# A planner's clock with other constants, and another order of the first loads, in an fp32 encoder kernel

## The chip, the cores and the metric

The kernel runs on one core of a Trainium2 chip. The metric is the device time of one execution in microseconds (us). The core has five engines that run side by side, each strictly in the order of its own program: TensorE (PE) multiplies matrices, with PEld for the loading of its stationary operand; VectorE (DVE) and ScalarE (ACT) do elementwise work; GpSimd (POOL) computes here only powers for norms; SyncE (SP) issues almost all DMAs. An engine waits for another by semaphores.

## What is computed

Two layers of an encoder, 256 tokens wide 1024, everything in fp32:

```python
def hybrid_layer(x, mem, ...):
    h = rms_norm(x, norm_mix_g)
    rq, rk, rv, rg, pv, nq, nk, nv, mq = jnp.split(h @ w_in, 9, axis=-1)
    ret = merge_heads(rms_norm(bidirectional_retention(rotary(rq), rotary(rk), rv), ret_norm_g)) * silu(rg)
    pool = multiscale_pool(pv, pool_w, pool_scale)
    na = neighbourhood_attention(rms_norm(nq), rms_norm(nk), nv, na_rpb)
    mk, mv = jnp.split(rms_norm(mem, norm_mem_g) @ w_mem_kv, 2, axis=-1)
    mo = memory_attention(rms_norm(mq), rms_norm(mk), mv)
    up = jnp.einsum('bsnc,ncd->bsnd', jnp.stack([ret, pool, na, mo], axis=2), w_branch)
    gates = sigmoid(h @ w_gate).reshape(b, s, N_BRANCH, dm)
    x = x + jnp.einsum('bsnd,bsnd->bsd', gates, up) @ w_out
    a, g = jnp.split(rms_norm(x, norm_ffn_g) @ w_ffn_in, 2, axis=-1)
    return x + (silu(a) * g) @ w_ffn_out
```

Each branch has 4 heads (or groups) of 64. The memory has 256 tokens.

## The kernel before

**Tiles.** The tokens are two tiles of 128 (t = 0, 1). Activations are turned (transposed on PE against an identity) so that they can be the stationary operand, and split in a high part, rounded by a cast to `fp32r`, and the low rest: `hhi`/`hlo` for normalized x, `bhi`/`blo` for branches, memory and the FFN's hidden block. Weights come as 272 slots of 512 KB (128 x 1024 fp32) and are split in the same way: ACT casts `raw` to `whi` (called a cast or a split below), DVE subtracts to get `wlo`. A product of two such pairs is three matmuls of 128x512, hi·hi, hi·lo and lo·hi, called three products below. A slot makes six products for each tile, in PSUM banks `A` (four) and `B` (two); `C` (two) is for turns. There are 4 `raw` buffers and 10 of each split. A slot's DMA is issued, on SP, right behind the subtraction that frees its `raw` buffer.

**Work beside the products.** The attention, retention, pooling, norm and FFN chains are Python generators. A chain issues a few instructions on ACT, DVE, POOL and PE (turns, scores, value products), then yields until its results are there. Among their steps: `to_heads` (about line 549) turns the heads of two sources into `C` and makes `ls`, `rs`, `rl` of them; `attention` makes scores in `B`, takes exponentials on ACT into `sc`, scales and turns them back (copies to `pt` for the first two heads, to `sc` for the second two), and multiplies with the values; `gate_chain` is a sigmoid on ACT; `hid_chain` (line 860) is a sigmoid on ACT and two DVE products, and `hid_T` turns the hidden block.

**What sets the order.** Nothing is ordered at run time. While the program is built, a model clock (class `Clock`, line 66) walks along: every instruction that is issued through the wrapper `Engine` gets a modelled start (after its operands, from a table of last reads and writes) and a modelled duration (`cost`, line 84). The main loop (line 1088) asks this clock which tile's next slot is `ready`; `background` resumes the chains whose time has come; `pump` (line 301) issues a slot's split when its weights have landed by the clock and when ACT or DVE is no more than a few microseconds behind PE by the clock. So the clock's constants decide in which place each cast, copy, sigmoid and turn stands in the order of its engine, and the chip then runs these orders as they are.

Before, the clock counts a product of 512 columns at 0.4167 ns a column and 13.5 ns, a transfer at 390 bytes per ns with 1.2 us ahead and 1.0 behind, 1.28 us for each change between exponential and sigmoid on ACT, and 0.2 us for each change of PE between its narrow fp32 products and others.

**The start** (`begin`, line 1007, and the lines from 1071) is written by hand. SP loads half of tile 0's x, slot 0 in two halves, slot 1, and so on; ACT's queue loads the identity and the first half of tile 1's x. PE runs some products on zeros, turns four blocks of tile 0, does the six products of slot 0 for tile 0, turns four blocks of tile 1, and does the six of slot 0 for tile 1.

Of the kernel before, what the change touches and what calls it, by code (L numbers as in the profile page):

```python
# [9 lines left out]
F32 = mybir.dt.float32  # L10
F32R = mybir.dt.float32r
AF = mybir.ActivationFunctionType
# [11 lines left out]
HD = 64  # L24
# [9 lines left out]
LEAD = 7  # L34
MAX_LAG = 8
WARM = 6.6
TABLE_LOAD = 1.28
WINDOW = (6, 4, 1.5, 0.4)
VERBOSE = False
BRANCHES = (2, 3, 0, 1)  # L40
# [3 lines left out]
class Engine:  # L44


    def __init__(self, real, clock, name):
        self.real, self.clock, self.name = real, clock, name

    def __getattr__(self, op):  # L50
        f = getattr(self.real, op)

        def call(*args, **kw):
            outs = [kw[k] for k in ("out", "accum_out") if kw.get(k) is not None]
            ins = [v for k, v in kw.items() if k not in ("out", "accum_out")]
            rest = list(args)
            if "out" not in kw:
                outs.append(rest.pop(0))
            func = next((v for v in rest if isinstance(v, AF)), None)
            self.clock.enter(self.name, op, outs, [v for v in ins + rest if isinstance(v, bass.AP)], kw, func)  # L60
            return f(*args, **kw)  # L61

        return call


class Clock:
# [5 lines left out]
    def __init__(self):  # L72
        self.at = dict.fromkeys(("PE", "ACT", "DVE", "POOL", "SP", "DMA"), 0.6)
        self.reads, self.writes = {}, {}
        self.mark = 0.0
        self.column = None
        self.narrow = False
        self.table = None

    @property  # L80
    def now(self):
# [2 lines left out]
    def cost(self, eng, op, outs, ins, kw):  # L84
        n = max([x.free_size() for x in outs[-1:] + ins[:1]])
        if eng == "PE":
            o = outs[0]
            n = o.free_size() * (2 if self.now < WARM else 1)
            narrow = op == "matmul" and ins[0].dtype == F32 and o.partition_size() == HD
            change = 0.2 * (narrow != self.narrow)  # L90
            self.narrow = narrow
            if op == "transpose":
                return n * 0.845e-3 + change
            if ins[0].dtype == F32R:
                return n * 0.4167e-3 + 0.0135 + change
            half = o.partition_size() == HD and o.base_partition()
            if o.partition_size() == HD:
                pair, self.column = self.column, None if half else n
                if half and pair == n:
                    return 0.02  # L100
            return max(n, 128) * 1.67e-3 + change
        if eng == "ACT":
            return 0.1 + n * 0.83e-3 + 0.1 * (kw.get("accum_out") is not None) + 0.04 * isinstance(kw.get("scale"), bass.AP)
        if eng == "POOL":
            if op == "memset":
                return 0.1 + n * 1e-3
            return 0.3 + 0.17 * n
        if op in ("tensor_copy", "tensor_scalar", "tensor_scalar_mul", "tensor_scalar_add", "memset"):
            return 0.085 + n * 0.6e-3
        return 0.08 + n * 1.045e-3 + 0.05 * (op == "scalar_tensor_tensor")  # L110

    def span(self, x):
        (stride, parts), *free = x.ap
# [12 lines left out]
        old = [r for r in table.get(key, ()) if r[4] > end - 60 and not (p0 <= r[0] and r[1] <= p1 and lo <= r[2] and r[3] <= hi)]  # L126
        table[key] = old + [(p0, p1, lo, hi, end, eng)]

    def enter(self, eng, op, outs, ins, kw, func=None):
        ins = [x for x in ins if x.space != bass.MemoryType.DRAM]  # L130
        outs = [x for x in outs if x.space != bass.MemoryType.DRAM]
        skip = "PE" if eng == "PE" else None
        t = max([self.last(self.writes, x) + self.LATENCY for x in ins]
                + [self.last(self.reads, x, eng) + self.LATENCY for x in ins if x.space == bass.MemoryType.PSUM]
                + [max(self.last(self.writes, x, skip), self.last(self.reads, x, skip)) + self.LATENCY for x in outs] + [self.at[eng]])
        if func in (AF.Exp, AF.Sigmoid) and func != self.table:
            self.table = func
            self.at["ACT"] += TABLE_LOAD
            t = max(t, self.at["ACT"])
        if op == "dma_start":  # L140
            self.at[eng] = t + 0.45
            t = max(self.at["DMA"], t + 1.2) + (outs + ins)[0].nbytes() / 390e3
            self.at["DMA"] = t
            end = t + 1.0
        else:
            end = self.at[eng] = t + self.cost(eng, op, outs, ins, kw)
        for x in ins:
            self.note(self.reads, x, end, eng)
        for x in outs:
            self.note(self.writes, x, end, eng)  # L150
        self.mark = max(self.mark, end)
# [9 lines left out]
def tile_encoder(ctx: ExitStack, tc: tile.TileContext, a: dict, out: bass.AP):  # L161
    clock = Clock()
    nc = Timed(tc.nc, clock)
# [184 lines left out]
    def start(gen, *reads):  # L348

        hold(*reads)  # L350
        chains.append([clock.now, gen])
# [655 lines left out]
    def begin():  # L1007

        parts = {(0, 0): (C[0], (0, 1)), (0, 1): (B[1], (2, 3)), (1, 0): (C[1], (0, 1)), (1, 1): (A[3], (2, 3)),
                 (0, 2): (C[0], (4, 5, 6, 7)), (1, 2): (C[1], (4, 5, 6, 7))}  # L1010

        def turn(t, *which):
            for c in which:
                bank, ks = parts[t, c]
                for i, k in enumerate(ks):
                    nc.tensor.transpose(bank[:, i * P:(i + 1) * P], X[t][:, k * P:(k + 1) * P], ident)

        def split(t, c):
            bank, ks = parts[t, c]
            ks = [(bank[:, i * P:(i + 1) * P], GAIN[0][0][:, k:k + 1], *act_h(t, k)) for i, k in enumerate(ks)]  # L1020
            for ps, g, hi, lo in ks:
                nc.scalar.activation(hi, ps, AF.Copy, scale=g)
            for ps, g, hi, lo in ks:
                nc.vector.scalar_tensor_tensor(out=lo, in0=ps, scalar=g, in1=hi.bitcast(F32), op0=ALU.mult, op1=ALU.subtract)
            if c:
                raise_flag(f"h{t}@0c{c - 1}")

        def weights():
            split_hi()
            split_lo()  # L1030

        state["by_hand"] = True
        warm(6)
        turn(0, 0, 1)
        warm(2)
        split(0, 0)
        weights()
        emit(0)
        turn(1, 0, 1)
        split(0, 1)  # L1040
        split(1, 0)
        emit(1)
        weights()
        split(1, 1)
        turn(0, 2)
        emit(0)
        turn(1, 2)
        split(0, 2)
        weights()
        emit(1)  # L1050
        split(1, 2)
        weights()
        emit(0)
        emit(1)
        state["by_hand"] = False
# [6 lines left out]
    with tc.manual_schedule():  # L1062
# [4 lines left out]
        def load_x(queue, t, c):  # L1067
            queue.dma_start(out=X[t][:, HALVES[c]], in_=a["x"][0, t * P:(t + 1) * P, HALVES[c]])
# [3 lines left out]
        load_x(nc.sync, 0, 0)  # L1072
        nc.scalar.activation(small[0], mhalf, AF.Square)
        clock.at["ACT"] += 1.2
        load_x(nc.scalar, 1, 0)
        issue_dmas(2)
        load_x(nc.sync, 0, 1)
        issue_dmas(3)
# [103 lines left out]
```

## Time and profile before

| | |
|---|---|
| three runs | 843.17 us median, 842.88 to 847.2 |
| profiled execution | 841.89 us, span 840.0 us |
| bytes moved | 152.86 MB, mean 182 GB/s |
| DVE, subtractions of weights | 275, 330.2 us busy |
| ACT, casts of weights | 273, 284.1 us busy |
| granted TensorE clock | 1.0 of full in the whole span |

The profile names operands by the program's names without buffer numbers; all compute stands under line 61, the wrapper's call. In the timeline a row has start, duration, engine, operation, output<-inputs, and in brackets the idle time of that engine just before, with what ended it. A row of PE longer than the distance to the next one is pipelining: the start of the next matmul, not the end of this one, shows the pace. An arrow in the view of waits reads "who waited <- for whom". A time against a name is when PE or an engine could not go on; idle time of ACT or DVE alone costs nothing.

### The profile page before, as it was taken

Reading aid. Unit: us, or ns where it says so; the run is one execution under the profiler, and the core shown is the slowest. Engines: PE = TensorE matmul, PEld = TensorE weight load, DVE = VectorE, ACT = ScalarE, POOL = GpSimd, SP = SyncE. Lnnn points to the kernel's source line nnn. Section 1 sums busy time; section 2 is a strip of 40 time slices with the busy share of each in tenths; the row PEclk is TensorE's granted clock in tenths of the full one; section 3 lists DMA queues with packets and bytes.
Section 4 is the critical chain, followed back from the end, with each engine's and each line's share of the span. In section 5 each row is a group of like instructions: output and inputs, shape, how many; then the busy total and the mean of one; then the engine's idle time right before and its main releaser. Section 6 shows DMA issues by size and latency. Waiting matters only on the chain.

```text
span 840.0 us, 10795 instructions
## 1 busy us (share of the span) xinstructions
PE 820.8 (98%) x3928; PEld 672.4 (80%) x3928; DVE 552.2 (66%) x802; ACT 470.1 (56%) x726; POOL 30.5 (4%) x32
## 2 busy tenths in 40 slices
PE   8999999999999999999999998999999999999998
PEld 6788778778887888888888877887888878888886
DVE  5898786865677556555568868584775765655541
ACT  6858887445465444444469677754444654444430
POOL 0400100000000000000011001000000000000000
PEclk9999999999999999999999999999999999999999
DMA  8946765546568656566374477446544676666611
GB/s 257 323 140 203 240 199 166 166 147 197 176 180 255 191 180 197 176 198 185 95 220 137 156 246 219 147 126 226 178 157 120 200 228 198 187 187 186 189 52 51
DMA packets 103765, 152.86 MB, mean 182 GB/s; under 512 B 6432, under 2 KB 55328, under 8 KB 103712
## 3 DMA queue, kind: packets, MB, share of 16 engines
q1 hardware_dynamic: 102848, 151.30, 57.1%
q10 hardware_dynamic: 864, 0.88, 0.3%
q8 instruction: 31, 0.51, 0.2%
q14 instruction: 22, 0.18, 0.1%
HBM read 151.10 MB, written 1.05 MB: 181 GB/s over the span
## 4 chain that ended last, share of the span: by engine, by line
PE 78%; ACT 7%; DMA 7%; DVE 6%; issue 2%; POOL 0%; SPq 0%; DVEq 0%; ACTq 0%; POOLq 0%
PE A L61 49%; PE B L61 25%; PE C L61 4%; DVE wlo L61 3%; ACT whi L61 2%; DMA raw<-in_w_in 2%; DMA mem<-in_pool_a 2%; DMA raw<-in_w_ffn_out 1%; DMA raw<-in_w_gate 1%; DVE w L61 1%; ACT rs L61 1%; ACT sc L61 1%; DMA raw<-in_w_mem_kv 1%; ACT qk L61 1%; ACT bhi L61 1%
## 5 line engine op out<-in xcount | busy, mean ns | idle before, releaser
L61 DVE TENSOR_TENSOR wlo<-raw,whi 128x1024 fp32r<-128x1024 f32 (+1 forms) x275 | 330.2, 1212 | 190.9 <-ACT whi L61 190.3
L61 ACT CAST whi<-raw 128x1024 fp32r<-128x1024 f32 (+1 forms) x273 | 284.1, 1050 | 214.0 <-PE A L61 83.0
L61 PE MATMUL A<-whi,hhi 128*128 128x512 f32 (+1 forms) x544 | 213.9, 393 | 1.6 <-ACT whi L61 0.7
L61 PE MATMUL A<-wlo,hhi 128*128 128x512 f32 (+1 forms) x544 | 208.9, 384 | 1.0 <-DVE wlo L61 1.0
L61 PE MATMUL A<-whi,hlo 128*128 128x512 f32 (+1 forms) x544 | 209.1, 384 | 0.0
L61 PEld LDWEIGHTS A<-whi,hhi 128*128 128x128 f32 x544 | 102.3, 188 | 23.2 <-issue 2.6
L61 PEld LDWEIGHTS A<-whi,hlo 128*128 128x128 f32 x544 | 102.2, 188 | 21.2 <-DVE hlo L61 0.8
L61 PEld LDWEIGHTS A<-wlo,hhi 128*128 128x128 f32 x544 | 102.5, 188 | 20.1 <-DVE wlo L61 2.0
L61 PE MATMUL B<-whi,hlo 128*128 128x512 f32 x288 | 112.5, 391 | 0.1
L61 PE MATMUL B<-whi,hhi 128*128 128x512 f32 x288 | 112.3, 390 | 0.0
L61 PE MATMUL B<-wlo,hhi 128*128 128x512 f32 x288 | 112.1, 389 | 0.0
L61 PE MATMUL A<-whi,bhi 128*128 128x512 f32 x272 | 108.3, 398 | 0.0
L61 PE MATMUL A<-whi,blo 128*128 128x512 f32 x272 | 106.2, 390 | 0.0
L61 PE MATMUL A<-wlo,bhi 128*128 128x512 f32 x272 | 106.1, 390 | 0.0
L61 PEld LDWEIGHTS B<-whi,hlo 128*128 128x128 f32 x288 | 54.0, 188 | 12.9 <-DVE hlo L61 1.8
L61 PEld LDWEIGHTS B<-wlo,hhi 128*128 128x128 f32 x288 | 54.1, 188 | 11.3
L61 PEld LDWEIGHTS B<-whi,hhi 128*128 128x128 f32 x288 | 54.1, 188 | 11.0
L61 PEld LDWEIGHTS A<-whi,blo 128*128 128x128 f32 x272 | 51.1, 188 | 11.0
L61 PEld LDWEIGHTS A<-whi,bhi 128*128 128x128 f32 x272 | 51.1, 188 | 10.4 <-issue 0.8
L61 PEld LDWEIGHTS A<-wlo,bhi 128*128 128x128 f32 x272 | 51.2, 188 | 9.7
L61 DVE SCALAR_TENSOR_TENSOR w<-B,rms,w 128x256 f32<-128x256 f32 x72 | 34.7, 482 | 3.9 <-ACT w L61 2.6
L61 ACT CAST bhi<-C 128x512 fp32r<-128x512 f32 x28 | 16.4, 586 | 34.4 <-PE C L61 34.3
(115 smaller groups left out, 605.5 us busy)
## 6 DMA issues: line engine op xcount, KB each, us to landing
raw<-in_w_ffn_in SPq DMA_DIRECT2D x176, 256.0 KB, 3.2
raw<-in_w_gate SPq DMA_DIRECT2D x64, 512.0 KB, 4.4
raw<-in_w_ffn_out SPq DMA_DIRECT2D x44, 512.0 KB, 3.9
raw<-in_w_in SPq DMA_DIRECT2D x35, 512.0 KB, 4.3
raw<-in_w_branch SPq DMA_DIRECT2D x16, 512.0 KB, 4.5
raw<-in_w_out SPq DMA_DIRECT2D x16, 512.0 KB, 4.2
raw<-in_w_mem_kv SPq DMA_DIRECT2D x8, 512.0 KB, 4.3
xn<-in_bias SPq DMA_DIRECT2D x4, 512.0 KB, 5.4
```

The source lines that it names most:

```text
L61: return f(*args, **kw)
```

## The change

The clock loses its two change costs (the function tables of ACT, narrow products of PE), counts a 512-column product at 0.416 ns a column and 3 ns, a transfer at 280 bytes per ns with 1.1 us ahead and 0.9 behind, 0.48 us instead of 0.45 for a DMA's issue, and DVE's fixed parts at 70 ns instead of 80 or 85. At the start, the first half of tile 1's x goes to SP's queue, behind both halves of slot 0, and its four turns stand between the third and the fourth product of tile 0.

```diff
@@ Clock.cost
-            narrow = op == "matmul" and ins[0].dtype == F32 and o.partition_size() == HD
-            change = 0.2 * (narrow != self.narrow)
-            self.narrow = narrow
             if op == "transpose":
-                return n * 0.845e-3 + change
+                return n * 0.84e-3
             if ins[0].dtype == F32R:
-                return n * 0.4167e-3 + 0.0135 + change
+                return n * 0.416e-3 + 0.003
...
-            return max(n, 128) * 1.67e-3 + change
+            return max(n, 128) * 1.67e-3
...
-            return 0.085 + n * 0.6e-3
-        return 0.08 + n * 1.045e-3 + 0.05 * (op == "scalar_tensor_tensor")
+            return 0.07 + n * 0.55e-3
+        return 0.07 + n * 1.05e-3 + 0.05 * (op == "scalar_tensor_tensor")
@@ Clock.enter
-        if func in (AF.Exp, AF.Sigmoid) and func != self.table:
-            self.table = func
-            self.at["ACT"] += TABLE_LOAD
-            t = max(t, self.at["ACT"])
         if op == "dma_start":
-            self.at[eng] = t + 0.45
-            t = max(self.at["DMA"], t + 1.2) + (outs + ins)[0].nbytes() / 390e3
+            self.at[eng] = t + 0.48
+            t = max(self.at["DMA"], t + 1.1) + (outs + ins)[0].nbytes() / 280e3
             self.at["DMA"] = t
-            end = t + 1.0
+            end = t + 0.9
@@ begin
         weights()
+        def between():
+            turn(1, 0, 1)
+            return
+            yield
+        start(between())
         emit(0)
-        turn(1, 0, 1)
         split(0, 1)
@@ first loads
-        load_x(nc.scalar, 1, 0)
-        issue_dmas(2)
+        issue_dmas(1)
+        load_x(nc.sync, 1, 0)
+        issue_dmas(2)
```

`emit` runs the chains after the first of its two groups of three products, and so `between` puts the turns there.

What this does to the orders is shown at three places. The first is PE's start, before: `x_105` and `x_106` are tiles 0 and 1 of x, `A_61` and `A_63` their banks, `whi_73`/`wlo_83` slot 0.

```order
L61 MATMUL B_65<-w_125 128x128 x2
L61 MATMUL A_61<-whi_73,hhi_93 128x512
L61 MATMUL A_61<-wlo_83,hhi_93 128x512
L61 MATMUL A_61<-whi_73,hlo_95 128x512
L61 MATMUL A_61<-whi_73,hhi_93 128x512
L61 MATMUL A_61<-wlo_83,hhi_93 128x512
L61 MATMUL A_61<-whi_73,hlo_95 128x512
L61 MATMUL C_68<-ident_gain,x_106 128x128 x2
L61 MATMUL A_64<-ident_gain,x_106 128x128 x2
L61 MATMUL A_63<-whi_73,hhi_94 128x512
```

And with the change:

```order
L59 MATMUL B_65<-w_125 128x128 x2
L59 MATMUL A_61<-whi_73,hhi_93 128x512
L59 MATMUL A_61<-wlo_83,hhi_93 128x512
L59 MATMUL A_61<-whi_73,hlo_95 128x512
L59 MATMUL C_68<-ident_gain,x_106 128x128 x2
L59 MATMUL A_64<-ident_gain,x_106 128x128 x2
L59 MATMUL A_61<-whi_73,hhi_93 128x512
L59 MATMUL A_61<-wlo_83,hhi_93 128x512
L59 MATMUL A_61<-whi_73,hlo_95 128x512
L59 MATMUL A_63<-whi_73,hhi_94 128x512
```

The four turns of tile 1 have moved from behind the sixth product to behind the third.

The second place is ACT in layer 1, where the keys of the memory are evicted from `A_61` (tile 0) and `A_63` (tile 1): `qk_112` takes the values, `w_128` the squares of the keys for their norm, and the casts of weights stand between. Before:

```order
L61 CAST whi_80<-raw_72 128x1024
L61 CAST whi_81<-raw_69 128x1024
L61 CAST whi_82<-raw_70 128x1024
L61 ACTIVATE qk_112<-A_61,rms 128x256
L61 ACTIVATE w_128<-A_61,rms 128x256
L61 CAST whi_73<-raw_71 128x1024
L61 CAST bhi_99<-C_68 128x512
L61 ACTIVATE qk_112<-A_63,rms 128x256
L61 ACTIVATE w_128<-A_63,rms 128x256
L61 CAST whi_74<-raw_72 128x1024
```

With the change:

```order
L59 CAST whi_80<-raw_72 128x1024
L59 ACTIVATE qk_112<-A_61,rms 128x256
L59 ACTIVATE w_128<-A_61,rms 128x256
L59 CAST whi_81<-raw_69 128x1024
L59 CAST bhi_99<-C_68 128x512
L59 ACTIVATE qk_112<-A_63,rms 128x256
L59 ACTIVATE w_128<-A_63,rms 128x256
L59 CAST whi_82<-raw_70 128x1024
L59 CAST whi_73<-raw_71 128x1024
L59 CAST whi_74<-raw_72 128x1024
```

Two casts have moved from ahead of tile 0's eviction to behind it, one of them behind tile 1's. PE has the turn of these heads 24 products behind tile 1's last memory product in both. In the FFN of each layer the sigmoid of the second hidden block (`w_128<-A_63`, tile 1) has moved in the same way ahead of one cast, and DVE's two products with it ahead of one subtraction; its turn keeps its place, 15 products behind the block's last.

The third place is ACT in layer 0, where the exponentials of the second two neighbourhood heads (`sc_119`, `sc_120`) meet the first gate (`gt`, from `A_62` and `A_64`). Before:

```order
L61 CAST whi_78<-raw_70 128x1024
L61 ACTIVATE sc_119,sums_151<-sc_119,sums_151 128x256 x2
L61 ACTIVATE sc_120,sums_152<-sc_120,sums_152 128x256 x2
L61 ACTIVATE mem_123<-mem_123 128x512
L61 ACTIVATE sc_119<-sc_119,sums_151 128x256
L61 CAST whi_79<-raw_71 128x1024
L61 ACTIVATE sc_120<-sc_120,sums_152 128x256
L61 ACT_TABLE_LOAD
L61 ACTIVATE gt<-A_62,rms 128x512
L61 ACTIVATE gt<-A_64,rms 128x512
L61 COPY sc_119<-B_65 128x512
L61 ACT_TABLE_LOAD
```

With the change:

```order
L59 ACT_TABLE_LOAD
L59 ACTIVATE gt<-A_62,rms 128x512
L59 CAST whi_79<-raw_71 128x1024
L59 ACT_TABLE_LOAD
L59 ACTIVATE sc_119,sums_151<-sc_119,sums_151 128x256 x2
L59 ACT_TABLE_LOAD
L59 ACTIVATE gt<-A_64,rms 128x512
L59 ACT_TABLE_LOAD
L59 ACTIVATE sc_120,sums_152<-sc_120,sums_152 128x256 x2
L59 ACTIVATE mem_123<-dist,lg 128x512
L59 ACTIVATE sc_120<-sc_120,sums_152 128x256
L59 CAST whi_80<-raw_72 128x1024
```

The gates have moved between the exponentials, with two table loads more. On PE, 24 products stand between the last gate product (`A_64`) and the turn of `sc_119`, and three more before that of `sc_120`; before, the gate products ended at the same row and the turn of `sc_119` came 9 products after.

Elsewhere the same kinds of swaps: in layer 0 the memory's first turn stands 27 products later (120 of them before it instead of 93), and the loads of the pooling matrix one slot earlier in SP's order. In the opening, ACT has the square of the first block (`w_125<-A_61`) ahead of the seventh cast and the evictions of the second ahead of the ninth. In the steady part of the FFN, from its third hidden block on, the orders of PE, ACT and DVE are as before.

More of the change, by code (lines that the diff above doesn't have):

```diff
@@ L36 @@
 WARM = 6.6
-TABLE_LOAD = 1.28
 WINDOW = (6, 4, 1.5, 0.4)
@@ L58, in call @@
                 outs.append(rest.pop(0))
-            func = next((v for v in rest if isinstance(v, AF)), None)
-            self.clock.enter(self.name, op, outs, [v for v in ins + rest if isinstance(v, bass.AP)], kw, func)
+            self.clock.enter(self.name, op, outs, [v for v in ins + rest if isinstance(v, bass.AP)], kw)
             return f(*args, **kw)
@@ L76, in __init__ @@
         self.column = None
-        self.narrow = False
-        self.table = None
     @property
@@ L127, in note, with enter @@
         table[key] = old + [(p0, p1, lo, hi, end, eng)]
-    def enter(self, eng, op, outs, ins, kw, func=None):
+    def enter(self, eng, op, outs, ins, kw):
         ins = [x for x in ins if x.space != bass.MemoryType.DRAM]
```

## The prediction

> **What bounds the kernel now.** First the busy times, from the profile's page:
>
> ```profile
> span 840.0 us, 10795 instructions
> PE 820.8 (98%) x3928; PEld 672.4 (80%) x3928; DVE 552.2 (66%) x802; ACT 470.1 (56%) x726; POOL 30.5 (4%) x32
> ```
>
> TensorE (PE) sets the time. How dense it is when nothing disturbs it stands in the chain of waits, in the FFN of layer 0:
>
> ```profile
> 288.36 10.88 PE B L61 x48
> ```
>
> 48 products in 10.88 us, 0.2267 us each. Neither their number nor their shapes change, so the change can only move PE's waits. The view of waits, for PE alone, gives them all (us in total, times, longest):
>
> ```profile
> PE C L61 <- DVE w L61: 7.6, 5, 3.0
> PE C L61 <- DVE blo L61: 1.8, 2, 1.6
> PE B L61 <- DMA mem<-in_pool_a: 1.8, 3, 1.1
> PE B L61 <- DVE mhalf L61: 1.0, 1, 1.0
> PE A L61 <- DVE wlo L61: 1.0, 3, 0.5
> PE A L61 <- ACT whi L61: 0.7, 1, 0.7
> PE A L61 <- DVE xn L61: 0.6, 1, 0.6
> PE A L61 <- ACT hhi L61: 0.2, 1, 0.2
> ```
>
> They sum to 14.7 us. That is the whole stake: a gain ends near 1.7%, a loss has no such end.
>
> **The change part by part.**
>
> **1. The start.** The stretch before:
>
> ```profile
> 1.23 0.39 ACTq L61 DMA_DIRECT2D x<-in_x  x1
> x<-in_x ACTq DMA_DIRECT2D x1, 256.0 KB, 4.6
> 7.08 0.62 ACT L61 CAST whi<-raw 128x512 fp32r<-128x512 f32 x1 [0.75 <-DMA raw<-in_w_in]
> 7.44 0.40 PE L61 MATMUL A<-whi,hlo 128*128 128x512 f32 x1
> 8.82 0.41 PE L61 MATMUL A<-whi,hlo 128*128 128x512 f32 x1
> 9.90 0.50 PE L61 MATMUL A<-whi,hhi 128*128 128x512 f32 x1 [0.24 <-ACT hhi L61]
> 11.35 0.39 PE L61 MATMUL A<-whi,hlo 128*128 128x512 f32 x1
> ```
>
> Half of tile 1's x lands at 1.23 + 4.6 = 5.83 us, the second weight half at 7.05: they share the engines. With x behind the weights the two landings change places, about 5.8 for the half and 7.05 for x. Then the second cast starts when the first ends, near 6.3, and x is there before the third product starts (the row at 7.44). The four turns follow at 7.7, products four to six at 8.1 to 8.6 (the sixth was at 8.82, with the turns still to come), and while they run ACT makes tile 1's high parts, so the wait in the row at 9.90 goes. Six products of tile 1 from 8.8 put the last at 8.8 + 5 × 0.227 = 9.9, against 11.35: **1.4 us less**. Bounds: 0.3 (x late, only the turns hidden) to 1.7 (the first cast gains too). ACT loses one issue of 0.39 us at a time when it waits anyhow; SP gains one, which pushes the second slot's issue back by some 0.45 us, hidden because ACT splits that slot only after tile 1's first parts, which the product at 9.90 waits for. The Trainium skill ("DMA: Bandwidth & Descriptors", the section on issuing engines not being separate queues) says that DMAs from SP and ACT run on the same 16 engines and interleave. By it moving x to SP wins nothing by itself, only its later place does; the landings of 5.83 and 7.05 agree.
>
> **2. Splits that no longer stand before a chain.** ACT runs in order. The new clock gives a 512 KB transfer 1.1 + 1.87 + 0.9 us instead of 1.2 + 1.34 + 1.0, so splits are put later in ACT's queue. In layer 0's FFN (second hidden block):
>
> ```profile
> 259.74 1.05 ACT L61 CAST whi<-raw 128x1024 fp32r<-128x1024 f32 x1 [1.66 <-DMA raw<-in_w_ffn_out]
> 260.69 0.47 ACT L61 ACTIVATE w<-A,rms 128x256 f32<-128x256 f32 x1
> 261.96 1.00 DVE L61 SCALAR_TENSOR_TENSOR w<-A,rms,w 128x256 f32<-128x256 f32 x2
> 263.01 0.55 PE L61 MATMUL C<-ident_gain,w 128*128 128x128 f32 x3 [1.68 <-DVE w L61]
> 676.94 0.33 PE L61 MATMUL C<-ident_gain,w 128*128 128x128 f32 x1 [0.96 <-DVE w L61]
> ```
>
> The sigmoid stands behind a cast whose weights come late; PE waits 1.68 us for what follows. Now the sigmoid stands ahead of that cast, whose weights are needed far later. Its product is complete before 258 (the turn is 15 products behind it), so it ends near 258.5, DVE's pair near 260.3, before PE comes at 261. The same swap in layer 1 removes the 0.96. **1.7 + 1.0 us less**, bounds half to all of it; what is late next there is nothing within a microsecond.
>
> The longest wait is in layer 1, at the turn of the memory heads:
>
> ```profile
> 501.29 1.05 ACT L61 CAST whi<-raw 128x1024 fp32r<-128x1024 f32 x1 [2.61 <-DMA raw<-in_w_branch]
> 505.56 1.05 ACT L61 CAST whi<-raw 128x1024 fp32r<-128x1024 f32 x1 [1.63 <-PE A L61]
> 506.88 0.47 ACT L61 ACTIVATE w<-A,rms 128x256 f32<-128x256 f32 x1
> 514.73 0.52 PE L61 MATMUL C<-ident_gain,w 128*128 128x128 f32 x3 [2.99 <-DVE w L61]
> 497.35 8.18 PE A L61 x35
> ```
>
> PE's run of 35 ends at 505.53; tile 0's memory product is six earlier, 504.2. The square of it waits until 506.88 behind two casts, and everything after (reduce, POOL's power, scale, then the same for tile 1) hangs on it. Both casts now stand behind it: it starts near 504.7, **2.0 us less** of 2.99 (bounds 1.0 and 3.0); the rest stays, since the two powers run one after the other.
>
> In layer 0 the same place costs 1.32 + 0.69:
>
> ```profile
> 100.08 0.30 PE L61 MATMUL C<-ident_gain,w 128*128 128x128 f32 x1 [1.32 <-DVE w L61]
> 101.07 0.52 PE L61 MATMUL C<-ident_gain,w 128*128 128x128 f32 x3 [0.69 <-DVE w L61]
> ```
>
> One cast goes out of the way there, but two decay exponentials come in: I take 0.8 (0 to 2.0). Layer 0's first turn waits 1.58 for the memory's low parts; these are now made 27 products later, when ACT is less full: 1.0 (0 to 1.6). The wait for xn: 0.3 (0 to 0.6). The pooling products have three more products ahead of them in layer 1 (0.68 us), and in layer 0 their load is issued one weight slot earlier: 1.0 of the 1.8 (0 to 1.8). **Together 3.1 us less.**
>
> **3. What the clock no longer sees.** Loads of ScalarE's function tables are not counted any more, so the planner mixes sigmoids and exponentials: two loads more in layer 0 (12 against 10). Durations, mean of each form:
>
> ```profile
> L61 ACT ACT_TABLE_LOAD x10 | 12.8, 1283 | 1.3 <-PEq L1171 1.2
> L61 ACT ACTIVATE gt<-A,rms 128x512 f32<-128x512 f32 x32 | 21.7, 688 | 9.9 <-PE A L61 9.8
> L61 ACT ACTIVATE sc<-sc,sums 128x256 f32<-128x256 f32 x29 | 14.6, 506 | 14.7 <-DVE sums L61 14.7
> L61 ACT CAST whi<-raw 128x1024 fp32r<-128x1024 f32 x271 | 282.8, 1054 | 213.0 <-PE A L61 83.0 <-PE B L61 72.9 <-issue 22.6
> L61 ACT ACTIVATE mem<-dist,lg 128x512 f32<-128x512 f32 x4 | 3.0, 738 | 0.0
> ```
>
> From the end of tile 0's gate product ACT needs gate 0.69, cast 1.05, load 1.28, two exponentials 1.01, load 1.28, gate 0.69, load 1.28, two exponentials 1.01, decay 0.74, scale 0.51: 9.5 us. PE has 33 products and one group of turns before it wants the second score tile: 7.5 + 0.4. **New wait: 1.7 us** (0 to 3). Behind that scale stand a cast and the two copies for the value products; they end about when PE has done the six products ahead of these, so I book no second wait. In layer 1 an uncounted load and an exponential (1.28 + 0.62) stand before the query heads' copies, with 30 products for cover instead of 36: 0.5 (0 to 1.2). In layer 0 the next scores come 6 products after the turn instead of 15, with ACT's copy behind two casts: 0.8 (0 to 1.4). For places that I did not follow I add 1.5 (0 to 3): a plan with constants off by 5% (0.216 against the 0.2267 above) leaves waits of its own.
>
> The Trainium skill ("ScalarE: Activation LUTs", What ACT_TABLE_LOAD costs) puts a drain of about 1.38 us beside the 1.283 us load. The trace has none:
>
> ```profile
> 107.47 1.28 ACT L61 ACT_TABLE_LOAD   x1
> 108.77 1.27 ACT L61 ACTIVATE gt<-A,rms 128x512 f32<-128x512 f32 x2
> ```
>
> The next instruction starts 0.02 us after the load. By that rule of the Trainium skill the three loads above would cost 4.1 us more and the time come to 842.6; the row speaks against it, and I give that 2%.
>
> **The sum.** Less: 1.4 + 1.7 + 1.0 + 2.0 + 3.1 = 9.2. More: 1.7 + 0.5 + 0.8 + 1.5 = 4.5. Net 4.7 us. The profiled execution took 841.89 (span 840.0 and 1.9 around it) and would take 837.2; the median, 843.17, is 1.3 higher, and by it the forecast is **838.5**.
>
> **The rivals.**
>
> *The waits only move* (30%). ACT's and DVE's work does not shrink, and a chain helped at one turn may be late at the next: the two powers on POOL after 505 show such a series. Against it: ACT is idle nearly half the time. Then the start's 1.4 and little else stays: 841.8.
>
> *Late weights, slower* (14%). In the opening, splits of slots 5 to 9 now stand behind evictions that wait for PE (the first block's square before the seventh cast), where they ran ahead before. In the trace ACT waits for weights in that stretch:
>
> ```profile
> 23.02 1.05 ACT L61 CAST whi<-raw 128x1024 fp32r<-128x1024 f32 x1 [1.17 <-DMA raw<-in_w_in]
> 27.13 1.05 ACT L61 CAST whi<-raw 128x1024 fp32r<-128x1024 f32 x1 [1.89 <-DMA raw<-in_w_in]
> 28.84 2.35 DVE L61 TENSOR_TENSOR wlo<-raw,whi 128x1024 fp32r<-128x1024 f32 x2
> ```
>
> None reached PE, because the lead hid them. By my count about 1 us of lead is left for each; the loss begins where eviction plus DMA wait exceed that. Then 3.1 us of DMA wait and two splits of 1.05 + 1.18 come through: 7.5, the start and the memory turn (2.4) are lost, and the time is 838.5 + 9.9 = 848.4.
>
> *The start does not do what it says* (8%): the first cast starts only 0.19 us after the tile's own parts, so earlier weights may find PE unready. With 0.3 instead of 1.4: 839.6.
>
> **How the numbers follow.** The forecast has 46%, the drain 2%. Low end: every named wait goes (1.7 + 1.6 + 2.0 + 0.6 + 2.7 + 3.0 + 1.8 = 13.4) against 1.7 more: 831.5, which I shorten to 832, since not all upper ends come together. High end: sure gains 4.0 (2.7, 1.0 and 0.3) against 7.3 of new waits: 846.5. A measurement of this kernel tells 0.5% (4.2 us) from no change: faster means below 838.95, slower above 847.4. The forecast lies near that edge: of its 46% some 34 fall below, with 6 from cases in between and 5 from late gains in the others: faster 0.45, same 0.42, slower 0.13.
>
> **What would show it.** Right: the thirteenth product near 9.9 us; no PE wait for w in the second FFN turn of either layer; under 1.2 us at layer 1's memory heads; 12 table loads and a wait of 1 to 2 us of PE for the second score tile in layer 0's second pair of heads. Wrong: PE waits for wlo or whi between 15 and 40 us, waits that sum to 14 us or more, or a cadence other than 0.2267.

## The result, and the profile after

The changed kernel takes 830.48 us (median of four runs, 829.23 to 831.19) against 843.64 us of the kernel before (four runs, 842.88 to 847.20). The ratio is 0.9839 with a 95% interval of 0.9815 to 0.9863: 1.6% faster. The forecast was 838.5 us with a range of 832.0 to 846.5, so the sign was right, and the time fell 1.5 us below the range.

The profiled execution of the changed kernel took 830.14 us with a span of 828.4. From its page and from its chain of waits:

```profile
span 828.4 us, 10785 instructions
PE 819.9 (99%) x3928; PEld 674.1 (81%) x3928; DVE 552.8 (67%) x805; ACT 471.8 (57%) x725; POOL 29.4 (4%) x32
283.53 10.88 PE B L59 x48
```

PE's work is the same to 1 us, and the undisturbed pace is the same to the digit (48 products in 10.88 us; this row is from the chain). The span is 11.6 us shorter, so PE's waits must have gone. The view of waits for PE, complete:

```profile
PE B L59 <- ACT sc L59: 1.9, 1, 1.9
PE B L59 <- DVE mhalf L59: 1.0, 1, 1.0
PE A L59 <- DVE wlo L59: 0.7, 1, 0.7
PE C L59 <- DVE w L59: 0.5, 1, 0.5
PE C L59 <- DVE blo L59: 0.2, 1, 0.2
```

They sum to 4.3 us. Before they summed to 14.9 us: the prediction's 14.7 leaves out the last row of that view, 0.2 us for the load of the identity. So 10.6 of the 11.6 us are waits that went. The rows at the places of the prediction, from PE's timeline and, last, from the groups by line:

```profile
9.62 0.40 PE L59 MATMUL A<-whi,hlo 128*128 128x512 f32 x1
57.09 0.39 PE L59 MATMUL A<-wlo,hhi 128*128 128x256 f32 x1 [0.73 <-DVE wlo L59]
84.35 0.66 PE L59 MATMUL B<-ident_gain,sc 128*128 128x128 f32 x4 [1.94 <-ACT sc L59]
258.13 0.60 PE L59 MATMUL C<-ident_gain,w 128*128 128x128 f32 x4
506.32 0.52 PE L59 MATMUL C<-ident_gain,w 128*128 128x128 f32 x3 [0.53 <-DVE w L59]
L59 ACT ACT_TABLE_LOAD x12 | 15.4, 1283 | 1.4 <-PEq L1168 1.2
```

The last of tile 1's six first products starts at 9.62 (11.35 before). The turn of the second hidden block at 258.13 has no bracket: its 1.68 us are gone. Layer 1's memory heads wait 0.53 instead of 2.99. New are 1.94 for the second score tile of layer 0 and 0.73 for one low part. Why the hidden block's turn no longer waits, in ACT's timeline:

```profile
253.97 1.05 ACT L59 CAST whi<-raw 128x1024 fp32r<-128x1024 f32 x1 [0.55 <-DMA raw<-in_w_ffn_in]
254.93 0.47 ACT L59 ACTIVATE w<-A,rms 128x256 f32<-128x256 f32 x1
256.28 1.06 ACT L59 CAST whi<-raw 128x1024 fp32r<-128x1024 f32 x1 [0.88 <-DMA raw<-in_w_ffn_out]
```

The sigmoid runs at 254.93; the cast that still waits for its weights (0.88 us) now stands behind it. Before, it stood ahead, and the sigmoid ran at 260.69.

Two executions far from all others, one of `all_but_transfers` (1173 us, at a granted clock of 0.655) and one of the kernel before beside the first four runs (1671 us), are left out of the medians and ratios below.

### The profile page after: what moved, and what is told of

Its sections match the earlier page's. It is cut to its first block, busy times and chain, and to the rows that moved or that the text cites. A ratio compares the mean times of both kernels' runs of the same rounds, so it can differ in the third digit from the quotient of the medians.

```text
span 828.4 us, 10785 instructions
## 1 busy us (share of the span) xinstructions
PE 819.9 (99%) x3928; PEld 674.1 (81%) x3928; DVE 552.8 (67%) x805; ACT 471.8 (57%) x725; POOL 29.4 (4%) x32
## 4 chain that ended last, share of the span: by engine, by line
PE 93%; ACT 3%; DVE 2%; issue 1%; DMA 1%; POOL 0%; DVEq 0%; POOLq 0%; ACTq 0%
PE A L59 61%; PE B L59 27%; PE C L59 5%; ACT whi L59 1%; DVE wlo L59 1%; ACT L59 1%; DVE w L59 1%; DMA raw<-in_w_mem_kv 1%; DVE blo L59 1%; ACT sc L59 0%; ACT rs L59 0%; POOL sm L59 0%; ACT qk L59 0%; ACT bhi L59 0%; DVE rl L59 0%
```

## The experiments

The runs came in four groups, each on one chip beside the kernel before (start_only to product_only beside a median of 844.33 us, four_casts to start_and_transfers beside 843.89, filled_waits to rate_240 beside 843.45, the last four beside 844.45). Differences in us below are between medians of one group, unless another is named; the intervals are in the table. The kernels differ in the orders of their engines alone, but for the filled one.

| run | median us | ratio to before, 95% |
|---|---|---|
| start_only | 840.64 | 0.9961 (0.9942 to 0.9979) |
| clock_only | 832.61 | 0.9855 (0.9829 to 0.9881) |
| dma_only | 832.46 | 0.9858 (0.9830 to 0.9885) |
| product_only | 839.60 | 0.9936 (0.9910 to 0.9961) |
| four_casts | 836.87 | 0.9906 (0.9882 to 0.9931) |
| all_but_transfers | 834.99 | 0.9885 (0.9853 to 0.9918) |
| table_counted | 835.25 | 0.9888 (0.9863 to 0.9914) |
| start_and_transfers | 833.66 | 0.9869 (0.9844 to 0.9895) |
| filled_waits | 843.75 | 1.0003 (0.9983 to 1.0023) |
| gates_held | 829.87 | 0.9839 (0.9806 to 0.9872) |
| rate_330 | 832.13 | 0.9872 (0.9841 to 0.9903) |
| rate_240 | 833.96 | 0.9883 (0.9849 to 0.9918) |
| changed_again | 830.97 | 0.9851 (0.9820 to 0.9882) |
| clock_only_again | 832.45 | 0.9863 (0.9835 to 0.9892) |
| gates_held_again | 828.93 | 0.9828 (0.9798 to 0.9857) |
| before_again | 844.71 | 1.0007 (0.9983 to 1.0030) |

### Which part carries the gain

**The start alone**: the last two parts of the change's diff, `begin` and `first loads`, put into the kernel before.

> The kernel before with the new start alone (order of the first loads, four turns between the products); the clock as it was. Theory A (the start's gain is kept to the end): PE is 1.7 us earlier from the twelfth product on, as in the trace of the change, and the time is 1.7 us less than before. Rival (a lead won at the start is lost at the first wait that is set by loads, not by PE): the first waits grow by what the start won, and the time is within 0.5 us of before.

Measured 840.64, 3.7 us less (1.8 to 4.9 by the interval), against the rival and more than theory A said. In its profile the start wins 0.86 us (the last of the six products at 10.49), since the turns wait 0.64 us for x, and the span is 838.6, 1.4 shorter. Behind the start the orders of PE, ACT and DVE are the same as before, instruction by instruction. So whatever else the 3.7 us hold is either chance or waits that came out shorter behind an earlier start; which of the two stays open. This profile also held a surprise on the granted clock, told below.

**The clock alone**: the other hunks.

> The kernel before with all the new constants of the clock and the old start. Theory A: the parts add up, so 11.5 us less than before (13.2 less 1.7), with PE's waits near 5 us in sum. Rival (the plan needs the earlier start to have its weights in time): 4 us or more of new waits in the opening, so less than 8 us gained.

Measured 832.61, 11.7 less. Theory A held in time, and the new plan doesn't need the new start. In its profile PE's waits sum to 7.0 us, not to the 5 expected. Its orders of ACT and DVE are those of the changed kernel, instruction by instruction, and PE's differ at the start alone.

**The transfers' constants alone.**

```diff
-            self.at[eng] = t + 0.45
-            t = max(self.at["DMA"], t + 1.2) + (outs + ins)[0].nbytes() / 390e3
+            self.at[eng] = t + 0.48
+            t = max(self.at["DMA"], t + 1.1) + (outs + ins)[0].nbytes() / 280e3
...
-            end = t + 1.0
+            end = t + 0.9
```

> The kernel before with the clock's constants for transfers alone changed (280 bytes per ns, 1.1 and 0.9 us around it, 0.48 for the issue). Theory A (transfers counted slower put casts behind the chains' evictions on ACT, and that is where the waits went): at least 7 us less than before, and the waits at layer 1's memory heads and at the second hidden block's turn gone or under 0.6 us. Rival R (products counted 5% too cheap give every chain more cover on PE): under 2 us less.

Measured 832.46, 11.9 us less: these numbers by themselves do as much as the whole new clock. What is left of the waits for `w`, and the next row, in PE's view of waits for this kernel:

```profile
PE C L61 <- DVE w L61: 1.5, 1, 1.5
PE A L61 <- DVE wlo L61: 1.3, 5, 0.5
```

7.6 us in five waits have become 1.5 in one, at layer 1's memory heads (that one was expected under 0.6 and missed). At that place this kernel doesn't make the swap: 171 casts stand ahead of tile 0's square in ACT's order, as before, against 169 in the changed kernel. The hidden blocks' waits are gone.

**The product's cost alone** (0.416 ns a column and 3 ns instead of 0.4167 and 13.5).

> The kernel before with the clock's cost of a 512-column product alone changed (0.216 us instead of 0.2268). Rival R (cheap products on the clock give every chain some 5% more cover on PE): at least 6 us less than before. Theory A (the transfers' constants do it): within 2 us of before, and the 2.99 us at layer 1's memory heads still there.

Measured 839.60, 4.7 us less: between the two theories. From PE's timeline:

```profile
140.70 0.50 PE L61 MATMUL A<-whi,bhi 128*128 128x512 f32 x1 [1.88 <-ACT bhi L61]
515.17 0.52 PE L61 MATMUL C<-ident_gain,w 128*128 128x128 f32 x3 [0.33 <-DVE w L61]
```

Here, too, the 2.99 us at layer 1's memory heads went (0.33 left), against what I expected, but not by the same swap: 171 casts stand ahead of tile 0's square, as before, and the turn stands six products later on PE. That fits rival R's cover. A new wait of 1.88 took part of the gain back.

**All but the transfers' constants.**

> The changed kernel with the clock's constants for transfers as before (390 bytes per ns, 1.2 and 1.0 us, 0.45 us). Theory A (the transfers' constants carry the gain): at least 5 us slower than the changed kernel (835.5 or more), with waits of PE of 9 us or more. Rival (the other constants do as much, by two ways to one end): within 2 us of the changed kernel.

Measured 834.99: 8.9 faster than before, and 4.5 slower than the 830.48 of the changed kernel. Theory A asked for 5, and for 9 us of waits; they sum to 7.2. So it missed on both counts, and so did the rival, which said within 2 us. The old long waits are still there in part:

```profile
38.64 1.09 PE L61 MATMUL C<-ident_gain,w 128*128 128x128 f32 x8 [1.84 <-DVE blo L61]
509.35 0.52 PE L61 MATMUL C<-ident_gain,w 128*128 128x128 f32 x3 [1.68 <-DVE w L61]
```

The parts do not add up: 11.9 us by the transfers alone and 8.9 by all the rest make more than the 13.2 of both, because in part they remove the same waits (those at layer 0's memory heads are gone in both). The constants of DVE and the change costs were not run alone.

### Is it the casts ahead of the chains?

**Four casts held back by hand**, with the clock's constants and the start as before. The hold is in the planner, so the clock places some later instructions anew: three products stand behind each hidden block's turn instead of ahead of it, and from 515 to 600 us the orders of layer 1 differ from those before.

```diff
-VERBOSE = False
+VERBOSE = False; HOLD = {86: 249.8, 168: 492.5, 169: 495.2, 222: 655.0}
...
-            if (j < min(n_slots, state["free"] + NS, state["lo"] + NR) and soon(clock.at["ACT"], window)
+            if (clock.now >= HOLD.get(j, 0) and j < min(n_slots, state["free"] + NS, state["lo"] + NR) and soon(clock.at["ACT"], window)
```

> The kernel before with its own clock and start; only four casts of weights are held back in ACT's order: one behind the sigmoid of the second hidden block in each layer, two behind the squares of the memory heads in layer 1. Theory A (a cast ahead of a chain's step is the wait): the waits of 1.68, 0.96 and 2.99 us go to nothing, nothing and 0.5 us, so the span is 5.1 us shorter, and the median 5 to 7 us less, since in most runs of the kernel before the granted clock is a little under full (0.995), as it was around its longest wait in the trace of the run with the start alone. Rival (the waits only move): the three are gone but others of the same size appear, and the time is within 2 us of before.

Measured 836.87, 7.0 us less, and a span of 834.3, 5.7 shorter than 840.0. ACT's timeline in layer 1, then PE's row at the memory heads:

```profile
505.47 0.49 ACT L61 ACTIVATE w<-A,rms 128x256 f32<-128x256 f32 x1
505.82 2.97 ACT L61 CAST whi<-raw 128x1024 fp32r<-128x1024 f32 x3
510.72 0.52 PE L61 MATMUL C<-ident_gain,w 128*128 128x128 f32 x3 [0.51 <-DVE w L61]
```

The square stands ahead of the casts and the wait is 0.51, as expected. The waits at the two hidden blocks are gone, though their turns now come earlier. These three places give 5.1 of the 5.7 us of span. Holding four of 273 casts, with what the planner made of it, gives half of the whole gain. This is the strongest evidence for the mechanism of the prediction's second part, and against the rival that the waits only move.

The traces of the other runs say the same by a count of ACT's order. At layer 1's memory heads, 169 casts stand ahead of tile 0's square in nine profiles, and PE waits 0 to 0.76 us there. In seven others it is 170 or 171 casts, and PE waits 1.52 to 2.99 us. (The other two are the one with six more products of cover and one, told below, in which the wait was filled.) At the second hidden block of layer 0, 88 casts stand ahead of the sigmoid in six profiles, and PE waits 0.21 to 1.68 us; with 87 or 86, in the other twelve, it does not wait.

**How far back?** The rate of transfers in the changed kernel's clock, 280 bytes per ns, set to 330 and to 240.

> The changed kernel with transfers counted at 330 bytes per ns instead of 280. If the gain grows with how late the splits are put: between the 835.3 of 390 and the 830.5 of 280, about 833. If it is a matter of which swaps a plan happens to make: anywhere from 829 to 837, with other waits than either.

> The changed kernel with transfers counted at 240 bytes per ns instead of 280. If later splits go on helping: 830.5 or under. If they are late enough at 280: weights come late, PE waits for whi or wlo, 832 or more. If it is a matter of which swaps a plan happens to make: anywhere from 829 to 837.

With 390, 330, 280 and 240 the medians are 834.99, 832.13, 830.48 (830.97 in the last group) and 833.96: lowest at 280, as two of the expectations together had it. They come from different groups, and the intervals of neighbours overlap. Nor is it a smooth trend at each place: at 330 PE waits 2.54 us at layer 1's memory heads, more than the 1.68 at 390, so the expectation that each plan makes its own swaps is not refuted. At 240 PE waits 3.0 us for low parts; the longest two waits of this kernel behind its start:

```profile
65.55 0.39 PE L59 MATMUL A<-wlo,hhi 128*128 128x256 f32 x1 [1.22 <-DVE wlo L59]
89.29 0.55 PE L59 MATMUL B<-ident_gain,sc 128*128 128x128 f32 x3 [1.67 <-ACT sc L59]
```

That is the rival of late weights in another form: at 65 us no landing is late, but DVE has worked without a pause since 58 us on steps of chains that stand ahead of this subtraction. The wait of 0.73 us at 280 is of the same kind, so it begins there and grows beyond. The better number is not the truer one. From the page of the changed kernel, the median from issue to landing:

```profile
raw<-in_w_gate SPq DMA_DIRECT2D x64, 512.0 KB, 4.2
```

The clock's figure for it, when nothing queues ahead, is 3.5 us at 390, 3.9 at 280 and 4.2 at 240 (1.1 + 2.18 + 0.9).

### The table loads

**Tables counted again** in the changed kernel.

> The changed kernel, but function tables of ACT are counted on the clock as before (1.28 us a change). Theory A: ten loads, the wait of 1.94 us for the second score tile in layer 0 is gone and nothing else moves for the worse, so 828.5 us, 1.9 less than the changed kernel. Rival (any other plan has its own late places): within 0.7 us of the changed kernel or slower.

Measured 835.25, 4.8 us slower than the changed kernel. The wait of 1.94 is gone, but the plan is another one in all that follows. Its profile has 16 table loads, not the ten expected; why stays open. And it has a worse place (PE's timeline):

```profile
139.82 0.79 PE L61 MATMUL A<-whi,bhi 128*128 128x512 f32 x1 [2.25 <-ACT bhi L61]
141.58 0.80 PE L61 MATMUL A<-whi,blo 128*128 128x512 f32 x1 [0.54 <-DVE blo L61]
```

The branch's high part stands behind three casts there. In the windows the granted clock is 0.50 from 140 to 146 us, right behind this wait, so a part of the 4.8 us goes with the clock. Theory A fell: a term can be right, and still undoing its cause doesn't give it back.

**The two gates held back by hand** in the changed kernel. The orders of PE, ACT and DVE then differ from 73 to 134 us and nowhere else.

```diff
-        yield
+        yield HOLD.pop(t, 0)
         nc.scalar.activation(g, ps, AF.Sigmoid, scale=RH[t])
```

`HOLD` is (77.4,) on the clock for both tiles.

> The changed kernel, with the first two gates of layer 0 held back by hand until both second neighbourhood scores are scaled, so that ACT loads two tables fewer ahead of the second score tile. Theory A with C: the wait of 1.94 us is gone, and the 3 us at half clock behind it too: 1.9 to 3.2 us less than the changed kernel, 827.3 to 828.6, the fastest of all. Rival (the orders behind it, which differ in layer 0, bring another wait, as they did with tables counted throughout): 830 or more.

> The changed kernel with the two gates held back, again, beside the changed kernel on one chip. If the wait of 1.94 us is worth its length: 1.9 us under the changed kernel. If part of it comes back at the two score tiles behind (0.55 and 0.69 us in the first profile): 0.5 to 0.9 us under.

The first time it was 829.87, only 0.6 under the result above and between its two expectations, with two new waits of 0.55 and 0.69 and one for x. Beside the changed kernel on one chip it was 828.93 against 830.97, 2.0 less, and is the fastest of all. So there the wait was worth its length, by six executions of each, which overlap (828.0 to 831.7 and 830.4 to 832.5); the first group alone would have said otherwise. With the same orders, the waits of 0.55 and 0.69 were 0 and 0.20 in the second profile. In it the second score tile doesn't wait, and in ACT's timeline the load stands behind its scale:

```profile
80.87 0.51 ACT L59 ACTIVATE sc<-sc,sums 128x256 f32<-128x256 f32 x1 [0.35 <-DVE sums L59]
81.40 1.28 ACT L59 ACT_TABLE_LOAD   x1
```

In the same stretch of the changed kernel two loads stand ahead of that scale, which comes at 83.81:

```profile
78.91 1.28 ACT L59 ACT_TABLE_LOAD   x1
...
80.90 1.28 ACT L59 ACT_TABLE_LOAD   x1
...
83.81 0.49 ACT L59 ACTIVATE sc<-sc,sums 128x256 f32<-128x256 f32 x1
```

### The start

**Start and transfers together**, all other constants as before: the two diffs above.

> The kernel before with the new start and the transfers' constants, all else as before. If the two parts add up: 1.7 us less than with the transfers alone, 830.7 us, as fast as the whole change; the other constants then do nothing together. If the other constants help: 832 or more.

Measured 833.66, which is 832 or more, so the other constants do help. It is 1.2 more than with the transfers alone in another group, and the intervals overlap: no gain of the start can be seen here. Its profile, at the last of the six products and at both memory heads:

```profile
11.45 0.40 PE L61 MATMUL A<-whi,hlo 128*128 128x512 f32 x1
98.97 0.52 PE L61 MATMUL C<-ident_gain,w 128*128 128x128 f32 x3 [1.43 <-DVE w L61]
509.18 0.52 PE L61 MATMUL C<-ident_gain,w 128*128 128x128 f32 x3 [1.58 <-DVE w L61]
```

At 11.45 us it is no earlier than the old start. Layer 0's memory heads wait 1.43 us where the kernel with the transfers alone has no wait, though behind 32 us the two have the same orders. What differs there is a landing: ACT waits 2.61 us for the weights of its cast at 77.11, and 1.04 us at the same cast in the other profile, and runs 2 us later from there to the memory heads.

**The changed kernel and the new clock with the old start, again**, on one chip.

> The changed kernel unchanged, a second profiled execution. Theory D (what the new start wins hangs on when x and the first weights land and so differs between executions): the last of tile 1's first six products, at 9.62 us in the first profile, is at 10.4 us or later, and the median stays at 830 to 831. Rival (the start wins 1.7 us in each execution): it is at 9.5 to 9.9 again.

> The new clock with the old start, again, beside the changed kernel on one chip: the difference is what the start is worth. Theory D: 0.6 us (0 to 1.5) slower than the changed kernel, the mean of five profiled starts. Rival: 1.7 us or more.

830.97 against 832.45: the start is worth 1.5 us between these two, at the end of theory D's range. Some 0.6 of it is a wait at layer 0's memory heads that both profiles of the new clock with the old start have and the changed kernel hasn't. The last of the six is at 9.87 in this second profile of the changed kernel, so for this kernel the rival, a steady gain, was nearer than my theory. But the same hand-written start stands in ten profiles, and there this product is between 9.62 and 12.28 us (mean 10.79); in eight with the old start it is between 11.24 and 12.08 (mean 11.48). The mean gain is 0.7 us. What differs is when x lands, as the profile of the second run of the held gates shows:

```profile
8.85 0.44 PE L59 MATMUL C<-ident_gain,x 128*128 128x128 f32 x2 [1.57 <-DMA x<-in_x]
```

and for how long the first products start 0.43 us apart rather than 0.23 (until 7 us in the first profile of the changed kernel, until 10 in that of start and transfers together). Why the changed kernel itself was early both times stays open.

### The clock behind a wait

The profile of the run with the start alone, at layer 1's memory heads: PE's timeline, and below it the windows (their last three columns are granted clock, DMA share and GB/s):

```profile
512.49 0.52 PE L61 MATMUL C<-ident_gain,w 128*128 128x128 f32 x3 [2.73 <-DVE w L61]
...
514.25 0.63 PE L61 MATMUL A<-wlo,hhi 128*128 128x512 f32 x1
514.67 0.63 PE L61 MATMUL A<-whi,hlo 128*128 128x512 f32 x1
```

```profile
510.00:512.00 2.00, 0.00 (x0) 0.00 (x0) 0.99 (x3) 1.58 (x2) 1.55 (x1) 1.00 0.67 205
514.00:516.00 2.00, 2.00 (x7) 1.52 (x6) 1.94 (x3) 1.80 (x3) 0.00 (x0) 0.50 0.70 171
```

Behind the wait the granted clock is 0.50, and products start 0.43 us apart instead of 0.2267. About seven do so, which costs some 1.4 us on top of the wait (7 × 0.20). In the first profile of the kernel before, the clock stayed at 1.0 behind the wait of 2.99. From this came theory C.

**Two waits filled** in the kernel before.

```diff
+                    for _ in range(fill[t] if bank is C[1] and r == 0 else 0):
+                        nc.tensor.real.matmul(half(bank)[:, r, t * P:(t + 1) * P], ident, ident, start=True, stop=True)
                     nc.tensor.transpose(half(bank)[:, r, t * P:(t + 1) * P], src[t][:, r * P:(r + 1) * P], ident)
...
```

At the memory heads `fill` is (4, 2) in layer 0 and (0, 9) in layer 1, and elsewhere 0. The waits there fell to 0.31, 0.25 and 0.30 us.

> The kernel before, with products of the identity by itself put into the bank of the turn while PE waits there (nothing reads them, the turn writes over them): 4 and 2 at the memory heads of layer 0, 9 at those of layer 1, some 0.22 us each, so about 0.9, 0.4 and 2.0 us of the waits of 1.32, 0.69 and 2.99 us. The operations that are waited for start as before. Theory C (PE idle for about 2 us makes the granted clock fall to half for some 3 us, and this happened in most runs of the kernel before): the granted clock is 1.0 or 0.999 in nearly all runs and the median 1.5 to 2.5 us under before. Rival (the dips of the clock have another cause than these waits): the clock stays at 0.995 to 0.998 and the time is that of before or up to 0.5 us more.

Measured 843.75, ratio 1.0003: no gain. The clock was at 0.998 or less in 8 of 12 runs. In the profile the two filled places have no stretch under full clock behind them; there is one behind two waits for the pooling matrix, of 1.20 and 0.56 us:

```profile
583.78 0.78 PE L61 MATMUL B<-mem,qk 128*64 128x136 f32 x12 [0.56 <-DMA mem<-in_pool_a]
```

```profile
586.00:588.00 2.00, 2.00 (x9) 0.85 (x10) 0.00 (x0) 0.07 (x1) 0.00 (x0) 0.50 0.00 0
```

So theory C, as far as it named these two waits, fell.

**The kernel before, profiled again.**

> The kernel before unchanged, a second profiled execution. Theory C in its weaker form (a group of waits of about 2 us of PE can throw the granted clock to half for some 3 us, at whichever wait it happens to be): if the mean clock is under 0.998, the windows show each stretch under full clock right behind a wait of the views, and with each the products behind it start 0.43 us apart. Rival (the dips come on their own): stretches under full clock in the FFN's steady part, where PE doesn't wait.

The mean clock of this profile was 0.997. The only stretch under full clock before the end is again right behind a wait, now at the turn of layer 1's second hidden block. ACT's timeline, PE's, and a window:

```profile
674.32 1.05 ACT L61 CAST whi<-raw 128x1024 fp32r<-128x1024 f32 x1 [2.03 <-DMA raw<-in_w_ffn_out]
675.28 0.47 ACT L61 ACTIVATE w<-A,rms 128x256 f32<-128x256 f32 x1
677.60 0.90 PE L61 MATMUL C<-ident_gain,w 128*128 128x128 f32 x3 [2.17 <-DVE w L61]
678.73 0.63 PE L61 MATMUL A<-wlo,hhi 128*128 128x512 f32 x1
679.15 0.63 PE L61 MATMUL A<-whi,hlo 128*128 128x512 f32 x1
```

```profile
678.00:680.00 2.00, 2.00 (x7) 1.62 (x6) 2.00 (x3) 0.69 (x2) 0.00 (x0) 0.50 0.83 257
```

The weak form of theory C held, and the clock records of all 18 profiles bear it out: between the start and the last 10 us of the span they have eight stretches at 0.50, and each begins at the end of a wait of PE or at most 1.2 us behind it. But it is a chance: of the twelve waits of 1.8 us or more, six have such a stretch behind them and six, the 2.99 among them, have none. The rows show one thing more: this wait was 0.96 us in the first profile. The cast ahead of the sigmoid waited 0.76 us for its weights then and 2.03 now, and PE paid for it. A chain behind a cast inherits the scatter of a transfer.

## Why the prediction was right in kind and wrong in size

**What bounds it, and the stake.** Right: PE's pace did not change, and 10.6 of the 14.9 us of waits went. Not right is that the waits are the whole stake: what the granted clock loses behind them comes on top. Each sign that the prediction named for being right came in the first profile (its "thirteenth product" is the twelfth, the last of tile 1's first six).

**The start.** Forecast 1.4 less; 1.7 and 1.5 in the two profiles of this kernel, a mean of 0.7 over ten with this start. Not the cause of the miss.

**The swaps.** The two hidden blocks, 1.7 and 1.0, came as forecast. Layer 1's memory heads gave 2.46 of 2.99, where I took 2.0. The four held casts and the count over the profiles show that these swaps are the cause.

**First failing step: "Together 3.1 us less".** For layer 0's memory heads, layer 0's first turn, xn and the pooling I took 0.8, 1.0, 0.3 and 1.0 out of waits of 2.0, 1.6, 0.6 and 1.8. All of them are gone, 6.0 us. The halving had no row behind it, only caution; this is 2.9 of the miss of 8.0.

**Second failing step: "For places that I did not follow I add 1.5"**, with 0.5 and 0.8 for two chains in layers 1 and 0. Of these 2.8 us one wait of 0.73 came; the two chains wait for nothing. That is 2.1 more. The table loads, forecast at 1.7 and 12 loads, measured 1.94 (2.47 in the second profile) and 12: the one new wait that had been worked out from rows was right, though not what follows it, since in both profiles the clock falls to half behind it.

**Third failing step: "the median, 843.17, is 1.3 higher".** I carried the distance between profile and median over to the changed kernel. There it is 0.3, which is 0.9 of the miss. In 73 runs of the kernel before, by the granted clock of each run: at 0.999 or 1.0 the median is 840.9 us (9 runs), from 0.996 to 0.998 it is 843.5 (35), at 0.995 or less 845.5 (29). The profile that I worked from, at 1.0, was one of the few without such a stretch. The changed kernel was at 0.998 or above in all of its ten runs; its five at 1.0 have a median of 830.8. At full clock the change is thus worth some 10 us, about the waits that went; the other 3 of the 13 go with the clock. That fewer waits are why the clock falls less is argued from where its stretches stand; filling the waits at two places did not show it.

**What is left of the miss.** The three steps make 5.9 of 8.0 us. Another 0.5 is a wait for a low part in layer 1 (at 470.52 us before), which the prediction did not name and which went too, and 0.5 is what the memory heads and the start gave above the forecast, less what the score tile took. For about 1 us the cause stays open.

**The rivals.** "The waits only move" (30%) fell in this kernel, though in the one with tables counted it is what happened. Late low parts came at 240 bytes per ns, with 0.64 us at 36 us, in the opening, and 1.22 us at 65 us: the point from which they decide lies beyond 280. The low end of 832.0 failed too: all upper ends together, 831.5, lacked what the clock adds. The high end took 7.3 of new waits where its own upper bounds make 8.6 (3 + 1.2 + 1.4 + 3), which did not matter here.

**The place of the new constants.** I put the gain down to the transfers' constants, and alone they do give 11.9 us; but the rest alone gives 8.9, which the prediction did not consider. It does so in part by other means: at layer 1's memory heads one of the two casts moves, and the second hidden block's turn in layer 0 comes three products later, with 0.84 us of its wait left.

## What to carry to other kernels

Where engines run fixed orders, look for an instruction that waits for a transfer and stands ahead of a chain that PE waits for: holding back four such casts was worth half of this change. Discount a removed wait only by a row that shows what is late next, and count on a wait of some 2 us costing more than its length at times. A planner's constants are best chosen by a small series on the chip, not by how true they are, and before carrying a profile over to a median look at the granted clock of both. One profile is one execution: with the same orders, a wait here differed by 1 us and more from one execution to the next.

## What was unexpected of the hardware

The granted clock fell to half behind waits shorter than expected. In the second profile of the changed kernel it does so behind the score tile's wait:

```profile
85.12 1.04 PE L59 MATMUL B<-ident_gain,sc 128*128 128x128 f32 x4 [2.47 <-ACT sc L59]
86.38 0.63 PE L59 MATMUL A<-wlo,bhi 128*128 128x512 f32 x1
86.81 0.63 PE L59 MATMUL A<-whi,blo 128*128 128x512 f32 x1
```

Products stand 0.43 us apart until 88. In the first profile the clock is 0.50 from 86 to 88 us, behind the 1.94. Other such stretches stand behind 1.88 (the product's cost alone), 2.17, 2.25 and 2.73 us, and behind 1.41 and 0.69 us with one turn between (the run with the start alone, at 100 us), while the 2.99 us of the first profile left the clock at 1.0. The Trainium skill ("TensorE: Matmul & The Clock Gate", What's actually happening) describes a gate that halves the clock after an idle window of about 3.4 us, the window running free of the kernel; half clock and the chance in it agree with these rows, but a wait did not have to be 3.4 us long.

The second is how much a landing scatters between executions: x at the start made PE wait for nothing up to 1.57 us in profiles with one and the same start.
